# Output projection on four PSUM banks, residual tokens in other places of SBUF, and the first FFN products ahead of the last transposes

## The chip, the cores and the metric

The kernel runs on one core of a Trainium2 chip. The core has five engines with a queue of instructions each: TensorE (PE in the profile, with its weight loads as PEld), VectorE (DVE), ScalarE (ACT), GpSimd (POOL) and SyncE (SP), which here only issues transfers. They share the SBUF memory, and the matmul accumulators in PSUM, which has eight banks here, each of 512 fp32 numbers a partition. The metric is the device time of one execution in microseconds (us).

## The reference

One step of a hybrid decoder layer, for 1024 prompt tokens and 64 sample tokens (8 sequences of 8) that share the weights; the model width is 1024, the FFN width 2816. The part that the change touches is the tail of the layer, cut here to its core:

```python
# layer(): after attention, pooling and memory branches
merged = ga * (o @ w_br_attn) + gb * (pool_out @ w_br_pool) + gm * (om @ w_br_mem)
x = x + merged @ w_out                                   # output projection, residual
f, conv_state = conv_ffn(rmsnorm(x, norm2_g), conv_prefix, w_gate, w_up, conv_w, conv_b, w_down)
x = x + f

def conv_ffn(h, prefix, w_gate, w_up, conv_w, conv_b, w_down):
    g = h @ w_gate
    u = h @ w_up
    ext = concatenate([prefix, g], axis=1)
    gc = conv_b + sum(conv_w[j] * ext[:, j:j + L] for j in range(3))
    f = (gelu(gc) * u) @ w_down
    return f, ext[:, -2:]
```

All values are fp32. The outputs are the final normed tokens of both groups, keys and values, and the states.

## The kernel before, in words

**How fp32 products are made.** Each fp32 operand is split in two parts, hi and lo, by `split` (L109 ACT casts the hi part, L110 DVE subtracts it to get lo), and a product is three matmuls (`PASSES`: hi-hi, hi-lo, lo-hi) per 128 rows of the contraction. `put` takes 128 tokens by 512 columns of the normed residual, transposes them by four matmuls with the identity (L106), and splits the result into a right-hand operand of 128 by 512 tokens.

**Output projection (L917 to L994).** The residual tokens sit in eight tiles `x1[t]` of 128 tokens by 1024 columns and one tile `x1s` of 64 sample tokens; SP loads them (L949, L951) behind the weights. `w_out` is worked in two column halves, nb = 0 and 1. In each half the sample tokens come first (`mm_s`, L195, 16 matmuls) and then eight token tiles (`mm_n`, L187, 24 matmuls each). Each result bank is taken by `nat()`, which has two banks. `add_sq` adds the bank to the residual (L926, DVE), and ACT squares the sum with a running total (L927) and puts the squares, as scratch, into the same bank; only then is the bank free for the next tile but one.

In the second half each tile goes on: GpSimd's queue stores it to DRAM (L971, `x1_d`), `norm2` makes the scale (L931 and L116 to L122) and scales it in place (L933; it overwrites what the store reads, so it waits for the store to land), and `put` brings it into the FFN's operands. The FFN's gate and up products are a Strassen-like form with seven products for eight: the tokens are taken in pairs (even, odd), the columns in halves, which gives operands B11, B21 (of even tiles), B22 (of odd ones) and four more, T1 to T4, which are transposes of differences. The four differences of a pair (L982 to L985) are made in place, one after the other, two on DVE (L982, L984) and two on GpSimd (L983, L985), DVE and GpSimd in turn. T1 and T2 are filled as the pairs come; T3 and T4 are filled last, eight `put`s in `late`. Before that point `put` has two PSUM banks, called tp and av, which `tpb()` gives in turn.

**FFN gate and up (L996 to L1149).** For each of 22 blocks m of 256 weight columns (gate and up in turn), `prep(m)` makes the seven weight operands: four sums and differences on GpSimd (L1081, L1085, L1094, L1098, each into a tile `stm`, of which there are three) and seven splits (tiles wA to wD). It also does the sample tokens (`sample_ffn`: L1032, 16 matmuls per block, with a transposition of the 64 by 256 result). `products(m)` runs seven groups of 12 matmuls (L1109, `prod`) into one pair of banks `big` (halves a and b) and one bank `nat` (c): a11 on B11, s1 on T1, s2 on T2, a12 on B21, s3 on T3, s4 on B22, a22 on T4. ACT copies (`nc.scalar.copy`) and DVE additions (`acc`, L1125) bring the partial sums out of the banks. The `s3` group goes on adding into half a, and may start only when what stood there has been copied.

**What sets the order.** The program is written tile by tile, and a scheduler of the tile framework sets the order in each engine's queue; each queue then runs strictly in that order, with waits on semaphores. So the PE order of before and of the change need not be the order of the source. Pools of SBUF (`p5` for the residual tokens, `fa` for the FFN's working tiles, `pB` for the B operands) are given addresses one after the other, and a tile whose address belonged to a tile of a closed pool waits for the last use of what stood there.

Of the kernel before, what the change touches and what calls it, by code (L numbers as in the profile page):

```python
# [32 lines left out]
def hybrid_step(ctx, tc, x_prompt, x_sample, mem_prompt, cache_k, cache_v, page_table, state_pool,  # L33
# [868 lines left out]
    pB_cm = tc.tile_pool(name="pB", bufs=1, reuse_waits="tile")  # L902
# [12 lines left out]

    with tc.tile_pool(name="p5", bufs=1, reuse_waits="tile") as p5:
# [3 lines left out]
        nc.sync.dma_start(g2b, bc(norm2_g[0], P))  # L920
# [21 lines left out]
        raws = {}  # L942
        T1 = T2 = None
        todo, late = [], []
        for nb in range(2):
# [19 lines left out]
            for i, t in enumerate((0, 2, 1, 3, 4, 6, 5, 7) if nb else range(NT)):  # L965
                pt = nat()
# [15 lines left out]
                nc.vector.tensor_tensor(xa[:, 0:512], xb[:, 0:512], xa[:, 0:512], op=ALU.subtract)  # L982
                nc.gpsimd.tensor_tensor(xb[:, 0:512], xb[:, 512:D], xb[:, 0:512], op=ALU.subtract)  # L983
                nc.vector.tensor_tensor(xb[:, 512:D], xb[:, 512:D], xa[:, 0:512], op=ALU.subtract)  # L984
# [8 lines left out]
        T3, T4 = [ap_.tile([P, 2, 4, 512], F32R, tag="act", bufs=4, name=f"T{q}") for q in (3, 4)]  # L993
        for (xa, xb, a) in late:  # L994
            put(T3, xb[:, 0:512], a)
            put(T4, xa[:, 512:D], a)  # L996

    with tc.tile_pool(name="fa", bufs=1, reuse_waits="tile") as fa:
        def stm():
            return fa.tile([P, 4, P], F32, tag="stm", bufs=3, name=f"stm{uid()}")  # L1000

# [8 lines left out]
        def gu():  # L1010
            return fa.tile([P, T], F32, tag="gu", bufs=6, name=f"gu{uid()}")

        def conv(g, f):
            nc.gpsimd.tensor_copy(gc[:, f], g[:, T - 2:T])
            out = gu()
            nc.scalar.activation(out, g, AF.Identity, bias=cwb[:, f, 3:4], scale=cwb[:, f, 2:3])
            nc.vector.scalar_tensor_tensor(out[:, 1:], g[:, 0:T - 1], cwb[:, f, 1:2], out[:, 1:], op0=ALU.mult, op1=ALU.add)
            nc.vector.scalar_tensor_tensor(out[:, 2:], g[:, 0:T - 2], cwb[:, f, 0:1], out[:, 2:], op0=ALU.mult, op1=ALU.add)
            nc.scalar.activation(out, out, AF.Gelu_apprx_tanh)
            return out  # L1020

        def conv_s(out, e, f):
            nc.vector.tensor_scalar(out, e[:, :, 0:DS], cwb[:, f, 0:1], cwb[:, f, 3:4], op0=ALU.mult, op1=ALU.add)
            nc.vector.scalar_tensor_tensor(out, e[:, :, 1:1 + DS], cwb[:, f, 1:2], out, op0=ALU.mult, op1=ALU.add)
            nc.vector.scalar_tensor_tensor(out, e[:, :, 2:2 + DS], cwb[:, f, 2:3], out, op0=ALU.mult, op1=ALU.add)

        def sample_ffn(m, raw):
            j, c0 = m // 2, (m // 2) * 256
            pt = tpb()
            for k in range(KT):  # L1030
                r = (k % 2) * TS
                nc.tensor.matmul(pt[r:r + TS, 0:256], xs[:, k, 0:TS], raw[k // 4][:, k % 4], start=(k < 2), stop=(k >= 6),  # L1032
                                 tile_position=(0, r))
            gs = fa.tile([TS, 256], F32, tag="gs", bufs=2, name=f"gs{m}")
            nc.scalar.copy(gs, pt[TS:P, 0:256])
# [258 lines left out]
```

## Time and profile before

| what | value |
|---|---|
| median of 3 runs | 1833.76 us (1833.25 to 1834.86) |
| the profiled execution's own time | 1830.01 us |
| its span (first to last instruction in the profile) | 1828.2 us |
| PE busy | 1746.8 us, 96% of the span |
| DVE, ACT, POOL busy | 902.6, 716.9, 390.3 us |
| granted TensorE clock, mean | 0.98 of full |

The page divides the span into 40 slices of 45.7 us; the output projection and the start of the FFN lie between 918 and 1085 us, in the slices 21 to 24. A row of the timeline gives the start, the busy time, the engine, the line, what is written and read, the count, and in brackets how long the engine had been idle before and who released it. Names in rows leave out buffer numbers: `x` is one of the residual tiles, `B` and `T` the FFN's operands, `hl` a split weight tile, `nat`, `big`, `tp`, `av` the PSUM banks. "PEclk" in a table of windows is the granted clock of TensorE in that window, as a share of full speed.

### The profile page before, as it was taken

To read this page: it belongs to the slowest core of one execution; us is meant where nothing else is said; L and a number is where in the kernel's file an instruction comes from. 1 tells how busy PE (TensorE), PEld (TensorE's weight loads), DVE (VectorE), ACT (ScalarE), POOL (GpSimd) and SP (SyncE) were. 2 spreads that over 40 slices of the span, in tenths; PEclk is the share of its full clock that TensorE was granted. 3 is DMA by queue.
4 is the path that set the end of the run, shared out by engine and by line. 5 is a ranking of instruction groups with operands and counts; after the bars stand their busy time and mean duration, and the time that the engine had idled before them with its cause. 6 is when DMAs were issued, how large, how long until landed. Compare 5 with 4: busy or idle time off the path is not lost.

```text
span 1828.2 us, 22933 instructions
## 1 busy us (share of the span) xinstructions
PE 1746.8 (96%) x8285; PEld 1337.9 (73%) x8285; DVE 902.6 (49%) x1543; ACT 716.9 (39%) x1397; POOL 390.3 (21%) x427
## 2 busy tenths in 40 slices
PE   7999999998999999969989799999999999999997
PEld 5887876765776777747768667777777777788876
DVE  6421135221121676666725776666666666436464
ACT  5331235231221666655413353333334434334343
POOL 1113020302001242102200244443333342000000
PEclk9999999999999999969989999999999999999999
DMA  7341260557566342154442132222222223746663
GB/s 278 132 149 57 82 198 24 150 186 247 195 199 189 90 123 77 55 164 141 162 155 75 58 60 70 70 71 70 70 71 70 70 71 118 248 140 208 206 218 117
DMA packets 137367, 234.74 MB, mean 128 GB/s; under 512 B 25679, under 2 KB 71533, under 8 KB 137253
## 3 DMA queue, kind: packets, MB, share of 16 engines
q1 hardware_dynamic: 122117, 187.16, 32.3%
q0 software_dynamic: 15136, 46.12, 6.7%
q8 instruction: 65, 1.06, 0.2%
q14 instruction: 49, 0.40, 0.1%
HBM read 182.74 MB, written 50.54 MB: 128 GB/s over the span
## 4 chain that ended last, share of the span: by engine, by line
PE 78%; issue 8%; DVE 5%; DMA 4%; ACT 2%; POOL 2%; SPq 1%; POOLq 0%; DVEq 0%; ACTq 0%
PE big L1109 17%; PE nat L178 15%; PE big L1222 10%; PE nat L1109 7%; PE nat L187 5%; PE big L178 4%; PE nat L1222 3%; PE tp L1032 3%; PE tp L106 3%; PE av L106 2%; PE av L805 2%; PE nat L195 2%; PE big L775 1%; PE av L542 1%; DMA raw<-in_w_in 1%
## 5 line engine op out<-in xcount | busy, mean ns | idle before, releaser
L178 PE MATMUL nat<-act,hl 128*128 128x512 f32 x1344 | 352.1, 402 | 0.0
L178 PEld LDWEIGHTS nat<-act,hl 128*128 128x128 f32 x1344 | 243.2, 188 | 63.9 <-issue 14.0
L187 PE MATMUL nat<-hl,act 128*128 128x512 f32 x768 | 186.1, 400 | 9.9 <-ACT nat L927 8.2
L1222 PE MATMUL big<-wd,fh 128*128 128x512 f32 x792 | 187.5, 390 | 4.1 <-ACT big L1190 2.5
L187 PEld LDWEIGHTS nat<-hl,act 128*128 128x128 f32 x768 | 146.2, 192 | 42.0 <-ACT nat L927 8.6
L1222 PEld LDWEIGHTS big<-wd,fh 128*128 128x128 f32 x792 | 148.3, 188 | 36.3 <-ACT big L1190 3.4
L110 DVE TENSOR_TENSOR hl<-raw,hl 128x1024 fp32r<-128x1024 f32 x52 | 66.7, 1291 | 162.6 <-ACT hl L109 161.0
L1109 PE MATMUL big<-B,wA 128*128 128x512 f32 x528 | 130.6, 395 | 0.0
L110 DVE TENSOR_TENSOR wd<-wr,wd 128x1024 fp32r<-128x1024 f32 x66 | 84.5, 1282 | 74.0 <-ACT wd L109 71.9
L1109 PEld LDWEIGHTS big<-B,wA 128*128 128x128 f32 x528 | 97.4, 188 | 28.0 <-ACT gu L1134 8.2
L109 ACT CAST wd<-wr 128x1024 fp32r<-128x1024 f32 x66 | 69.3, 1052 | 83.2 <-PE tps L1229 35.3
L110 DVE TENSOR_TENSOR wB<-stm,wB 128x512 fp32r<-128x512 f32 x44 | 50.4, 1147 | 73.4 <-ACT wB L109 73.4
L568 POOL DMA_DIRECT2D gl<-ev x48 | 26.2, 545 | 272.0 <-ACT ev L567 244.7
L567 ACT COPY ev<-nat 128x512 f32<-128x512 f32 x48 | 28.1, 585 | 130.3 <-PE nat L178 130.1
L109 ACT CAST hl<-raw 128x1024 fp32r<-128x1024 f32 x60 | 62.6, 1051 | 26.7 <-DMA raw<-in_w_in 10.6
L1109 PE MATMUL nat<-B,wC 128*128 128x512 f32 x264 | 69.9, 399 | 0.0
L1163 POOL TENSOR_TENSOR gu<-gu,gu 128x1024 f32<-128x1024 f32 x22 | 57.0, 2590 | 52.3 <-DVE gu L1125 22.5
L1222 PE MATMUL nat<-wd,fh 128*128 128x512 f32 x264 | 67.2, 389 | 0.0
L1109 PE MATMUL big<-T,wD 128*128 128x512 f32 x264 | 66.7, 401 | 0.0
L1098 POOL TENSOR_TENSOR stm<-rf,stm 128x512 f32<-128x512 f32 x22 | 28.6, 1300 | 169.6 <-DVE wB L110 169.6
L1109 PE MATMUL big<-T,wC 128*128 128x512 f32 x264 | 64.6, 393 | 0.0
L1109 PE MATMUL nat<-T,wB 128*128 128x512 f32 x264 | 64.1, 390 | 0.0
(420 smaller groups left out, 3089.5 us busy)
## 6 DMA issues: line engine op xcount, KB each, us to landing
wr<-in_w_ffn_down SPq DMA_DIRECT2D x66, 512.0 KB
raw<-in_w_in SPq DMA_DIRECT2D x40, 512.0 KB
kr<-in_cache_k SPq DMA_DIRECT2D x64, 256.0 KB
vr<-in_cache_v SPq DMA_DIRECT2D x64, 256.0 KB
gl<-ev POOLq DMA_DIRECT2D x48, 256.0 KB, 3.1
rf<-in_w_ffn_gate SPq DMA_DIRECT2D x22, 512.0 KB
rf<-in_w_ffn_up SPq DMA_DIRECT2D x22, 512.0 KB
f_d<-gu POOLq DMA_DIRECT2D x22, 512.0 KB, 3.0
```

The costliest lines, as they stand in the source:

```text
L106: nc.tensor.transpose(out, in_, ident[:n, :n])
L109: nc.scalar.copy(hi, src)
L110: (lo_eng or nc.vector).tensor_tensor(lo, src, hi.bitcast(F32), op=ALU.subtract)
L178: nc.tensor.matmul(out, wf(k, pw)[:, n0:n0 + P], acts[c][ph][:, k, :], start=(k == ks[0] and (pw, ph) == (0, 0)), stop=(k == ks[-1] and (p ...
L187: nc.tensor.matmul(out, acts[c][ph][:, k, o:o + P], wf(k, pw), start=(k == ks[0] and (pw, ph) == (0, 0)), stop=(k == ks[-1] and (pw, ph) = ...
L195: nc.tensor.matmul(out, stack[:, k, :], wf(k, pw), start=(k == ks[0] and pw == 0), stop=(k == ks[-1] and pw == 1))
L805: nc.tensor.matmul(av[:, :P], aT[:, k * P:(k + 1) * P], vn[:, k0 + k], start=(k0 + k == 0), stop=(k0 + k == i))
L1032: nc.tensor.matmul(pt[r:r + TS, 0:256], xs[:, k, 0:TS], raw[k // 4][:, k % 4], start=(k < 2), stop=(k >= 6), tile_position=(0, r))
L1098: nc.gpsimd.tensor_tensor(s4, a12, s2, op=ALU.subtract)
L1109: nc.tensor.matmul(out, wt[:, pw, k], Bt[:, ph, k], start=(start and k == 0 and (pw, ph) == (0, 0)), stop=(k == 3 and (pw, ph) == (1, 0)), ...
L1163: nc.gpsimd.tensor_tensor(g[i], g[i], gts[i], op=ALU.mult)
L1222: nc.tensor.matmul(banks[i][nb], fh[:, ph, kk, i * P:(i + 1) * P], wh[:, pw, nb * 512:(nb + 1) * 512], start=(k == 0 and (pw, ph) == (0, 0 ...
```

## The change

Five things are done at once.

1. **Four banks for the projection.** `x1s` and the token tiles take their banks from `big()`, which has two pairs; two token tiles share one pair, and `x1s` takes the second half of a pair of its own. The sequence of pairs is x1s, (t0, t1), (t2, t3), and so on.
2. **`put` on four banks.** `put` takes in turn a bank of `nat()` and one of `tpb()`.
3. **Other homes.** `x1_5`, `x1_6`, `x1_7` are placed first in `p5`, then `x1s`, then the other tiles; `pB` moves to the other side of SBUF, so that `p5` and `fa` begin at other addresses; the load of the norm's gain `g2b` is written behind the loads of `x1`.
4. **Differences.** In all pairs but the last, all four differences are made by GpSimd; in the last pair (6, 7) they remain divided between DVE and GpSimd.
5. **Early products.** `prep` splits a12 together with a11, and `products` has a form `early` in which the groups a11 on B11 and a12 on B21 come first. For m = 0 and m = 1 these two groups (48 matmuls) are written ahead of the eight `put`s of T3 and T4. The helpers `stm`, `gu`, `conv`, `sample_ffn`, `prep`, `products` move ahead of the projection, unchanged but for this; the change in `g` at the end only fetches the two blocks begun early.

```diff
-    pB_cm = tc.tile_pool(name="pB", bufs=1, reuse_waits="tile")
+    pB_cm = tc.tile_pool(name="pB", bufs=1, side="right", reuse_waits="tile")
...
         tA = pair("wA")
         w["a11"] = piece(tA, 0, a11)
+        w["a12"] = piece(tA, 1, a12)
         yield
...
-            w["a12"] = piece(tA, 1, a12)
             smp_ = sample_ffn(m, raw)
...
+    def products(m, nxt, early=False):
...
         prod(a, w["a11"], B11, True)
+        if early:
+            prod(b, w["a12"], B21, True)
+            yield
+        g0, g1 = gu(), gu()
         nc.scalar.copy(hv(g0, 0), q(a))
...
-            prod(b, w["a12"], B21, True)
+        if not early:
+            prod(b, w["a12"], B21, True)
         acc(g0, 0, b)
...
     with tc.tile_pool(name="p5", bufs=1, reuse_waits="tile") as p5:
-        x1 = [p5.tile([P, D], F32, name=f"x1_{t}") for t in range(NT)]
+        x1 = [p5.tile([P, D], F32, name=f"x1_{t}") for t in (5, 6, 7)]
         x1s = p5.tile([TS, D], F32, name="x1s")
+        x1 = [p5.tile([P, D], F32, name=f"x1_{t}") for t in range(5)] + x1
         g2b = p5.tile([P, D], F32, name="g2b")
-        nc.sync.dma_start(g2b, bc(norm2_g[0], P))
...
+        pc = [0]
+
         def put(Bt, xh, a):
-            pt = tpb()
+            pc[0] += 1
+            pt = nat() if pc[0] % 2 else tpb()
...
             else:
+                nc.sync.dma_start(g2b, bc(norm2_g[0], P))
                 raws[0], raws[1] = raw_ffn(0), raw_ffn(1)
-            pt = nat()
-            mm_s(pt, wf, ms)
+            pt2 = big()
+            pt = pt2[:, 1]
+            mm_s(pt2[:, 1], wf, ms)
...
-                pt = nat()
+                if i % 2 == 0:
+                    pt2 = big()
+                pt = pt2[:, i % 2]
                 mm_n(pt, wf, macts, t)
...
-                nc.vector.tensor_tensor(xa[:, 0:512], xb[:, 0:512], xa[:, 0:512], op=ALU.subtract)
+                ve = nc.vector if i == 7 else nc.gpsimd
+                ve.tensor_tensor(xa[:, 0:512], xb[:, 0:512], xa[:, 0:512], op=ALU.subtract)
                 nc.gpsimd.tensor_tensor(xb[:, 0:512], xb[:, 512:D], xb[:, 0:512], op=ALU.subtract)
-                nc.vector.tensor_tensor(xb[:, 512:D], xb[:, 512:D], xa[:, 0:512], op=ALU.subtract)
+                ve.tensor_tensor(xb[:, 512:D], xb[:, 512:D], xa[:, 0:512], op=ALU.subtract)
                 nc.gpsimd.tensor_tensor(xa[:, 512:D], xa[:, 512:D], xb[:, 512:D], op=ALU.subtract)
...
         T3, T4 = [ap_.tile([P, 2, 4, 512], F32R, tag="act", bufs=4, name=f"T{q}") for q in (3, 4)]
+        pp = [prep(m) for m in range(2)]
+        pend = []
+        for m in range(2):
+            next(pp[m])
+            pend.append(products(m, prep(2) if m else pp[1], True))
+            next(pend[m])
         for (xa, xb, a) in late:
             put(T3, xb[:, 0:512], a)
             put(T4, xa[:, 512:D], a)
...
         for m in range(2 * NG):
-            nxt = prep(m + 1) if m + 1 < 2 * NG else iter(())
-            g = products(m, nxt)
-            for _ in nxt:
-                pass
+            g = next(pend[m] if m < 2 else products(m, prep(m + 1) if m + 1 < 2 * NG else iter(())))
```

The order that the scheduler makes of this is shown at three places. In these rows each name has its buffer number; the bracket lists the semaphores that the instruction waits on, by their owner.

**PE in the first column half, around the end of token tile 0.** `big1195`, not in the rows, holds the sample tokens' product, `nat1196` and `big1196` are the banks of token tiles 0 (and, with the change, 1); before, in `nat1195` stood the sample tokens' product. Before:

```order
L187 MATMUL nat1196_8897<-hl1194_8865,act1067_7999 128x512 x2
L187 MATMUL nat1196_8897<-hl1194_8865,act1068_8000 128x512
L187 MATMUL nat1196_8897<-hl1194_8865,act1067_7999 128x512
L187 MATMUL nat1197_8924<-hl1188_8850,act1067_7999 128x512 [waits Activation_49]
L187 MATMUL nat1197_8924<-hl1188_8850,act1068_8000 128x512
L187 MATMUL nat1197_8924<-hl1188_8850,act1067_7999 128x512 x2
```

With the change:

```order
L187 MATMUL big1196_8896<-hl1194_8864,act1067_7999 128x512 x2
L187 MATMUL big1196_8896<-hl1194_8864,act1068_8000 128x512
L187 MATMUL big1196_8896<-hl1194_8864,act1067_7999 128x512
L187 MATMUL big1197_8949<-hl1188_8849,act1067_7999 128x512 [waits Activation_49]
L187 MATMUL big1197_8949<-hl1188_8849,act1068_8000 128x512
L187 MATMUL big1197_8949<-hl1188_8849,act1067_7999 128x512 x2
L187 MATMUL big1196_8896<-hl1188_8849,act1067_7999 128x512 [waits Activation_49]
```

Before, token tile 1 follows tile 0 in the bank of x1s's product. With the change four matmuls of tile 2 (`big1197`, the pair that held x1s's product) stand between tile 0 and tile 1, and the first of them waits for ACT.

**GpSimd in the second column half, from the store of tile 5 to the first sum of FFN weights.** L971 and L1126 are the stores, L983 and L985 and L1138 to L1141 the differences, L1081 and L991 the first weight sum. Before:

```order
L971 DMA x1_d5_8822<-x1_5_8841 128x1024 [waits DMAHW6_49,DVE_49]
L971 DMA x1_d7_8824<-x1_7_8843 128x1024 [waits DMAHW0_49,DMASW5_49,DVE_49]
L983 TENSOR_TENSOR x1_5_8841<-x1_5_8841 128x512 [waits DVE_49]
L985 TENSOR_TENSOR x1_4_8840<-x1_4_8840,x1_5_8841 128x512 [waits DVE_49,Activation_49]
L983 TENSOR_TENSOR x1_7_8843<-x1_7_8843 128x512 [waits DVE_49]
L985 TENSOR_TENSOR x1_6_8842<-x1_6_8842,x1_7_8843 128x512 [waits DVE_49,PE_49,Activation_49]
L1081 TENSOR_TENSOR stm1286_9745<-rf00_9133,rf01_9135 128x512 [waits DMAHW1_49,PE_49,Pool_49]
```

With the change:

```order
L1126 DMA x1_d5_8822<-x1_5_8836 128x1024 [waits DMAHW5_49,DVE_49]
L1138 TENSOR_TENSOR x1_4_8844<-x1_5_8836,x1_4_8844 128x512 [waits DVE_49,PE_49]
L1139 TENSOR_TENSOR x1_5_8836<-x1_5_8836 128x512 [waits Pool_49]
L1140 TENSOR_TENSOR x1_5_8836<-x1_5_8836,x1_4_8844 128x512 [waits PE_49,Activation_49,Pool_49]
L1141 TENSOR_TENSOR x1_4_8844<-x1_4_8844,x1_5_8836 128x512 [waits Pool_49]
L1126 DMA x1_d7_8824<-x1_7_8838 128x1024 [waits DMAHW7_49,DMASW5_49,DVE_49]
L1139 TENSOR_TENSOR x1_7_8838<-x1_7_8838 128x512 [waits DVE_49]
L1141 TENSOR_TENSOR x1_6_8837<-x1_6_8837,x1_7_8838 128x512 [waits DVE_49]
L991 TENSOR_TENSOR stm1282_9800<-rf00_9129,rf01_9131 128x512 [waits DMAHW1_49,PE_49,Pool_49]
```

Before, the store of tile 7 stood ahead of all differences of pair (4, 5); now it stands behind four of them. The wait on PE of the first weight sum is, by the addresses, for the fourth of the eight late transposes before, and for the last of them (of tile 6) with the change.

**PE and DVE at the start of the FFN.** On PE, with the change, from the last projection matmul of tile 7 (`big1255`) to the first late transpose (`nat1274`); `big1270` is block 0, `big1272` block 1, and where a line is left out, three `put`s of the last pair stand between block 1's products:

```order
L187 MATMUL big1255_9533<-hl1207_9125,act1069_8001 128x512
L1018 MATMUL big1270_9671<-B11_8830,wA0_9666 128x512 [waits Activation_49]
L1018 MATMUL big1270_9671<-B11_8830,wA0_9666 128x512 x11
L1018 MATMUL big1270_9671<-B21_8831,wA0_9666 128x512 [waits Activation_49]
L1018 MATMUL big1270_9671<-B21_8831,wA0_9666 128x512 x11
L1018 MATMUL big1272_9706<-B11_8830,wA1_9701 128x512 [waits Activation_49]
...
L1018 MATMUL big1272_9706<-B11_8830,wA1_9701 128x512 x5
L1018 MATMUL big1272_9706<-B21_8831,wA1_9701 128x512 x12
L106 MATMUL nat1274_9732<-ident_72,x1_1_8841 128x128 [waits PE_49]
L106 MATMUL nat1274_9732<-ident_72,x1_1_8841 128x128 x3
```

Before, only the twelve matmuls of a11 on B11 of block 0 stood there. On DVE, from the first split of block 1's `wB` to the addition (`acc`) for which PE's group s3 of block 0 waits; before:

```order
L110 TENSOR_TENSOR wB1_9839<-stm1296_9840,wB1_9839 128x512 [waits Activation_49]
L110 TENSOR_TENSOR wB1_9839<-stm1297_9857,wB1_9839 128x512 [waits Activation_49]
L1036 TENSOR_TENSOR gs1_9885<-tp1298_9876,gs1_9885 64x256 [waits Activation_49]
L1125 TENSOR_TENSOR gu1294_9804<-gu1294_9804,big1292_9802 128x4x128 [waits PE_49]
L110 TENSOR_TENSOR wC1_9901<-stm1299_9902,wC1_9901 128x512 [waits Activation_49]
L110 TENSOR_TENSOR wC1_9901<-stm1300_9919,wC1_9901 128x512 [waits Activation_49]
```

With the change (the six rows of `fsv`, L932 to L934, between the third and the fourth are the sample tokens' convolution):

```order
L110 TENSOR_TENSOR wB1_9858<-stm1290_9859,wB1_9858 128x512 [waits Activation_49]
L110 TENSOR_TENSOR wB1_9858<-stm1291_9876,wB1_9858 128x512 [waits Activation_49]
L110 TENSOR_TENSOR wC1_9906<-stm1293_9907,wC1_9906 128x512 [waits Activation_49]
...
L110 TENSOR_TENSOR wC1_9906<-stm1294_9924,wC1_9906 128x512 [waits Activation_49]
L1033 TENSOR_TENSOR gu1288_9855<-gu1288_9855,big1270_9671 128x4x128 [waits Activation_49]
L945 TENSOR_TENSOR gs1_9902<-tp1292_9893,gs1_9902 64x256 [waits Activation_49]
```

Before, the addition stood ahead of both splits of block 1's `wC`; with the change it stands behind them, and these need the last of block 1's weight sums.

More of the change, by code (lines that the diff above doesn't have):

```diff
@@ L914, in raw_ffn, with stm, gu, conv @@
         return out
+    def stm():
+        return fa.tile([P, 4, P], F32, tag="stm", bufs=3, name=f"stm{uid()}")
+    def gu():
+        return fa.tile([P, T], F32, tag="gu", bufs=6, name=f"gu{uid()}")
+    def conv(g, f):
+        nc.gpsimd.tensor_copy(gc[:, f], g[:, T - 2:T])
+        out = gu()
+        nc.scalar.activation(out, g, AF.Identity, bias=cwb[:, f, 3:4], scale=cwb[:, f, 2:3])
+        nc.vector.scalar_tensor_tensor(out[:, 1:], g[:, 0:T - 1], cwb[:, f, 1:2], out[:, 1:], op0=ALU.mult, op1=ALU.add)
+        nc.vector.scalar_tensor_tensor(out[:, 2:], g[:, 0:T - 2], cwb[:, f, 0:1], out[:, 2:], op0=ALU.mult, op1=ALU.add)
+        nc.scalar.activation(out, out, AF.Gelu_apprx_tanh)
+        return out
@@ L1008, in hybrid_step @@
             nc.sync.dma_start(cwb[:, :, 3], ffn_conv_b[0].rearrange("(f p) -> p f", p=P))
[L1010 to L1020, printed above, removed]
@@ L1150, in hybrid_step @@
-        for _ in prep(0):
+        for _ in pp[0]:
             pass
@@ L1174, in hybrid_step @@
     pB_cm.__exit__(None, None, None)
-    with tc.tile_pool(name="fb", bufs=1, reuse_waits="tile") as fb:
+    with tc.tile_pool(name="fb", bufs=1, side="right", reuse_waits="tile") as fb:
         fr_b = [fb.tile([P, 2, 384], F32, name=f"fr{i}") for i in range(3)]
```

229 lines of the change are left out of this document (113 added, 116 removed).

## The prediction

> **What bounds the kernel now.** I read the page first: busy time, slices, and the chain that ended last.
>
> ```profile
> PE 1746.8 (96%) x8285; PEld 1337.9 (73%) x8285; DVE 902.6 (49%) x1543; ACT 716.9 (39%) x1397; POOL 390.3 (21%) x427
> PE   7999999998999999969989799999999999999997
> PE 78%; issue 8%; DVE 5%; DMA 4%; ACT 2%; POOL 2%; SPq 1%; POOLq 0%; DVEq 0%; ACTq 0%
> ```
>
> PE is the bound, so time can only come from where it stands still or runs at a lower clock. The change works between 918 and 1085 us, where the slices dip to 6. The timelines and windows of that stretch show two gaps; from 1059.6 on PE has none.
>
> ```profile
> 920.96 5.64 PE L187 MATMUL nat<-hl,act 128*128 128x512 f32 x24
> 934.76 1.65 PE L187 MATMUL nat<-hl,act 128*128 128x512 f32 x3 [8.16 <-ACT nat L927]
> 920.00:929.90 9.90, 6.46 (x27) 4.99 (x27) 3.12 (x5) 0.62 (x1) 0.00 (x0) 1.00 0.87 248
> 929.90:940.00 10.10, 5.24 (x12) 4.13 (x13) 2.06 (x3) 1.33 (x4) 0.00 (x0) 0.50 0.98 374
> 975.40:1033.80 58.40, 55.77 (x274) 44.99 (x274) 40.29 (x94) 18.15 (x44) 9.54 (x12) 1.00 0.26 94
> 1033.80:1042.50 8.70, 4.94 (x29) 3.57 (x27) 8.21 (x16) 2.58 (x7) 3.06 (x3) 1.00 0.15 61
> 1042.50:1059.60 17.10, 13.03 (x56) 9.00 (x56) 10.02 (x16) 8.48 (x15) 6.91 (x6) 0.50 0.37 5
> 1059.60:1085.00 25.40, 25.40 (x119) 18.87 (x116) 20.67 (x27) 14.34 (x27) 12.44 (x12) 1.00 0.28 85
> ```
>
> In a window row stand the window, its length, the busy time of PE, PEld, DVE, ACT and POOL, the granted clock, the DMA share and GB/s. **Gap 1:** token tile 0 ends at 926.6, and tile 1 waits 8.16 us for ACT's square of the sample tokens, which stands in its bank. The clock falls to 0.50 about 3.3 us after the stop: 12 matmuls took 5.24 us, 0.437 each. What the square waits for:
>
> ```profile
> 921.85 0.37 SPq L912 DMA_DIRECT2D rf<-in_w_ffn_gate  x1
> 922.45 0.34 SPq L920 DMA_DIRECT2D g2b<-in_norm_g  x1
> 922.85 0.48 SPq L949 DMA_DIRECT2D x1s<-in_x_sample  x1
> 928.72 0.33 SPq L951 DMA_DIRECT2D x<-in_x_prompt  x1
> 931.04 0.33 SPq L951 DMA_DIRECT2D x<-in_x_prompt  x1
> 932.38 0.33 SPq L951 DMA_DIRECT2D x<-in_x_prompt  x1
> SPq L951 <- DMA g2b<-in_norm_g: 2.0, 1, 2.0
> 932.41 1.40 DVE L926 TENSOR_TENSOR x1s<-x1s,nat 64x512 f32<-64x512 f32 x2 [8.60 <-DMA x1s<-in_x_sample]
> 933.98 0.59 ACT L927 ACTIVATE nat<-x1s 64x512 f32<-64x512 f32 x1 [10.90 <-DVE x1s L926]
> ```
>
> Three late issues of L951 go out as rf, g2b and x1s have landed: 928.7, 931.0, 932.4. So x1s lands last of three transfers, and from there to the next matmul pass 2.4 us (add, square). **Gap 2** begins at the end of the projection:
>
> ```profile
> 1033.67 2.43 PE L1109 MATMUL big<-B,wA 128*128 128x512 f32 x10
> 1039.30 0.63 PE L106 MATMUL tp<-ident,x 128*128 128x128 f32 x4 [1.82 <-DVE B L110]
> 1041.83 0.63 PE L106 MATMUL av<-ident,x 128*128 128x128 f32 x4 [1.90 <-DVE x L933]
> 1055.42 1.08 PE L106 MATMUL av<-ident,x 128*128 128x128 f32 x4 [0.64 <-POOL stm L1094]
> 1072.65 3.01 PE L1109 MATMUL big<-T,wC 128*128 128x512 f32 x12
> ```
>
> After the first products only transposes are left, on two banks, each waiting for the last tile's norm, its differences, or the split that frees a bank; from 1042.5 the clock is 0.50 here too. The last transposes end at 1056.5. The group s3 of block 0 starts at 1072.65: I use it as the mark to measure the change by.
>
> **The change part by part.** *Four banks and the load of g2b.* In the changed PE order, four matmuls of tile 2 in x1s's own pair stand ahead of tile 1, so PE still waits for the same square: the four banks don't free it here. On SP's queue the load of g2b moves behind the token loads, while the one of rf stays ahead. What is gained is g2b's time, 931.04 − 928.72 = **2.3 us**; x1s lands at 930.0, PE goes on at 932.4, and the stop of 5.8 us still halves the clock. Bounds: 0, if the token loads, now issued earlier, take that time, and 8.16 + 12 × (0.437 − 0.227) = 10.7, if PE could pass the square.
>
> *put on four banks, and the order in the second half.* Before, PE is idle 58.40 − 55.77 = 2.6 us there. The price of a transposition, and of a matmul at full clock:
>
> ```profile
> 991.51 0.60 PE L106 MATMUL tp<-ident,x 128*128 128x128 f32 x4
> 991.95 0.60 PE L106 MATMUL av<-ident,x 128*128 128x128 f32 x4
> 992.30 4.60 PE L187 MATMUL nat<-hl,act 128*128 128x512 f32 x19
> 1083.03 2.88 PE L1109 MATMUL nat<-T,wB 128*128 128x512 f32 x12
> 1085.75 0.62 PE L1109 MATMUL big<-T,wB 128*128 128x512 f32 x2
> ```
>
> Two transpositions take 0.79 us from 991.51 to 992.30, 0.40 each; twelve matmuls 2.72 us, 0.227 each. Three more transpositions stand ahead of the projection's end in the changed order: **+1.2 us**, moved only. The first matmul of tile 0 now waits for the square of tile 7 from the first half, **+0.6** (the square of 933.98 took 0.59).
>
> *Differences on GpSimd.* Rows beside each other:
>
> ```profile
> 1004.94 0.68 DVE L982 TENSOR_TENSOR x<-x,x 128x512 f32<-128x512 f32 x1
> 1005.87 1.30 POOL L983 TENSOR_TENSOR x<-x 128x512 f32<-128x512 f32 x1
> 1005.87 1.32 DVE L931 TENSOR_TENSOR ss<-ssn 128x1 f32<-128x1 f32 x1 [0.25 <-ACT nat L927]
> 1021.79 0.56 POOL L971 DMA_DIRECT2D x_d<-x  x1 [3.42 <-DVE x L926]
> 1025.62 1.28 DVE L933 SCALAR_TENSOR_TENSOR x<-x,rsy,g2b 128x1024 f32<-128x1024 f32 x1 [1.29 <-DMA x_d<-x]
> ```
>
> A difference is 1.30 us on GpSimd against 0.68 on DVE, so four in line are 5.2 us. Before, the pair from 1004.94 ended at 1010.3, 5.4 us with the handing over; the pair itself is no later. But the stores of tiles 3 and 7 now stand behind a whole pair in GpSimd's queue, tile 4's amid one, and from a store's issue to the scaling that waits for it are 3.8 us; the transpositions and PE come behind that. Also a DVE addition of one column with two SBUF inputs, whose like takes 0.16, took 1.32 beside the GpSimd difference that began with it. Bounds: nothing, if the store finds GpSimd free, and 7.8 = three stores, each behind half a pair (2.6). I take the middle, **+3.9 us**, as no row is nearer to either end. The projection then ends at 1033.8 − 2.3 + 1.2 + 0.6 + 3.9 = 1037.2.
>
> [...]
>
> *Early products.* 48 matmuls instead of 12 stand ahead of the late transpositions: 48 × 0.227 = 10.9 us. Three transpositions of the last pair among them (1.2), a stall for that pair's norm (0.5; before 1.90) and eight late ones on four banks make 16.6. Of these eight I take four at 0.40, with a bank free, and four at the pace of the split that frees one, 0.6 (DVE's 0.68, overlapping a little): 4.0. Before, on two banks and at half clock, ten intervals from 1041.83 to 1055.42 took 13.6, 1.4 each. So the last transposes end at 1037.2 + 16.6 = 1053.8.
>
> What follows hangs on GpSimd: the weight sums' tiles now lie where tiles 5 to 7 stood, and the first waits for the very last transposes, while before the first ran at 1051.49, five us ahead of them. The scheduler also puts the addition for which group s3 waits behind both splits of block 1's wC, so all eight sums must be made first.
>
> ```profile
> 1051.49 1.27 POOL L1081 TENSOR_TENSOR stm<-rf,rf 128x512 f32<-128x512 f32 x1 [5.09 <-issue]
> 1059.00 1.60 POOL L1098 TENSOR_TENSOR stm<-rf,stm 128x512 f32<-128x512 f32 x1 [3.66 <-DVE wB L110]
> 1059.38 1.77 DVE L110 TENSOR_TENSOR wC<-stm,wC 128x512 fp32r<-128x512 f32 x1
> 1063.94 1.15 POOL L1046 DMA_DIRECT2D out<-gs  x2
> 1071.90 0.69 DVE L1125 TENSOR_TENSOR gu<-gu,big 128x512 f32<-128x512 f32 x1 [0.59 <-PE big L1109]
> ```
>
> Where both engines work, a sum and a split go in turn, near 1.7 us a pair: 8 × 1.7 = 13.6, stores 1.15, the last split 1.3 (cast and subtraction, 0.6 and 0.7), the addition 0.7: **16.7 us** (14.3 if the sums go at 1.27 as alone, 18.5 if the three tiles for sums hold GpSimd up once more). Group s3 starts at 1070.5. Before, it started at 1072.65, but without 24 of the early matmuls (5.4) and with 5 of group s4 done (1.1): the same work was done at 1077.0. The lead is **6.5 us**.
>
> *What it costs later.* PE has some 10 us of work in those 16.7 (two blocks of sample matmuls, T1, T2), so it stands about 6. That may halve the clock once: 12 matmuls more at 0.437, **2.5 us** (0 to 5), and block 1's s3 can wait similarly, **1.2** (0.5 to 2.5). From block 2 on PE has the same order and no gaps; the other pool sides change no queue: 0.
>
> Sum: 6.5 − 2.5 − 1.2 = 2.8 us gained: 1830.0 becomes 1827.2 for the profiled execution. The runs' median lies 3.8 above it, so 1833.76 − 2.8 = **1831.0 us**.
>
> [...]
>
> **The rivals.**
> *A clean win.* GpSimd's chains are hidden (+0 instead of 3.9), the sums go at 1.27 (14.3 instead of 16.7), the clock stays and block 1 doesn't wait: 2.8 + 3.9 + 2.4 + 3.7 = 12.8 us gained, **1821.0**. For it: POOL is busy 9.54 of 58.40 us in the second half; against it: 1.60 and 1.77 beside each other.
> *Gap 1 doesn't shrink.* The token loads fill what g2b leaves, since the queues are at 0.98 of their share there: 0.5 gained, **1833.3**.
> *Slower.* GpSimd's queue decides: stores behind differences hold tiles 3, 4 and 7 back by 2.6 each (−3.9), the chain after the last transposes takes 18.5 (−1.8), and the idle time halves the clock for two such stretches (−2.5): 2.8 − 8.2 = −5.4, **1839.2**. It decides as soon as the three stores together come more than 6.7 us late at PE (3.9 + 2.8).
>
> **How the numbers follow.** The forecast has 0.45, the clean win 0.22, no smaller gap 0.14, slower 0.19. A measurement tells 0.2% (3.7 us) from no change here. The forecast's own range is 1827 to 1835; of its 0.45, 0.19 lie below 1830.1. Faster: 0.22 + 0.19 = 0.41; slower: 0.19 + 0.01 = 0.20; the same: 0.39. The range 1822 to 1838.5 leaves out half of the clean win and half of the slower case.
>
> **What would show it.** Right, if the stop after tile 0 is still there at some 5.8 us; the stores of tiles 3 and 7 start late behind L1141; the first L991 starts with the end of the last transposes, near 1054, and s3 of block 0 follows 16 to 17 us later behind an addition that DVE makes after wC. Wrong, if gap 1 vanishes, if DVE's splits aren't longer beside GpSimd's, or if s3 starts before 1066 or after 1076.

## The result, and the profile after

The changed kernel takes 1845.05 us (median of 5 runs, 1841.87 to 1848.76) against 1833.25 us, a ratio of **1.0064 [1.0047, 1.0081]**: slower by 0.64%, where 2.8 us of gain were forecast. Its profiled execution took 1841.87 us (span 1840.1), 11.9 us more than the one of before. One of the nine runs of e3 below is a slow one (2465.22 us at a mean granted clock of 0.652) and stays out of its ratio.

Busy time and the chain on the page of the changed kernel, which answer to those of before:

```profile
PE 1757.0 (95%) x8285; PEld 1335.8 (73%) x8285; DVE 903.1 (49%) x1537; ACT 717.3 (39%) x1397; POOL 400.8 (22%) x433
PE 82%; DVE 5%; DMA 4%; issue 3%; ACT 3%; POOL 2%; SPq 1%; DVEq 0%; POOLq 0%; ACTq 0%
```

PE has as many matmuls as before, and is busy 10.2 us longer: it does not only wait more, it works more slowly somewhere. Rows from the timeline of PE in the stretch that the change rewrites, with others between them left out:

```profile
920.19 5.64 PE L187 MATMUL big<-hl,act 128*128 128x512 f32 x24
930.84 34.96 PE L187 MATMUL big<-hl,act 128*128 128x512 f32 x144 [5.00 <-ACT big L1076]
1005.00 0.66 PE L106 MATMUL av<-ident,x 128*128 128x128 f32 x4 [1.16 <-POOL x L1140]
1011.95 0.66 PE L106 MATMUL nat<-ident,x 128*128 128x128 f32 x4 [0.70 <-POOL x L1138]
1027.26 1.19 PE L187 MATMUL big<-hl,act 128*128 128x512 f32 x4 [1.53 <-ACT big L1076]
1033.81 0.66 PE L106 MATMUL av<-ident,x 128*128 128x128 f32 x4 [1.00 <-POOL x L1138]
1036.85 1.11 PE L106 MATMUL nat<-ident,x 128*128 128x128 f32 x4 [1.68 <-POOL x L1140]
1039.46 6.68 PE L1018 MATMUL big<-B,wA 128*128 128x512 f32 x27
1056.20 0.63 PE L106 MATMUL av<-ident,x 128*128 128x128 f32 x4
1076.00 5.26 PE L1018 MATMUL big<-T,wC 128*128 128x512 f32 x12 [4.18 <-DVE gu L1033]
1118.93 2.92 PE L1018 MATMUL big<-T,wC 128*128 128x512 f32 x12
1550.42 3.03 PE L1018 MATMUL big<-T,wC 128*128 128x512 f32 x12
```

The last two rows are group s3 of block 2 and of block 21. In the kernel before they start so:

```profile
1117.26 2.93 PE L1109 MATMUL big<-T,wC 128*128 128x512 f32 x12
1545.51 3.01 PE L1109 MATMUL big<-T,wC 128*128 128x512 f32 x12
```

From block 2 on the order on PE is the same in both. PE doesn't stop again before FFN-down, and there it stops three times in either kernel, 4.08 us together before and 3.93 after. Yet the way to block 21 takes 431.49 us against 428.25, and from there to the end of the span 289.7 against 282.7. These two differences, 3.2 and 7.0, are **10.2 us of the 11.9**, far behind the place that the change is about. The table shows where each kernel's time lies, each from the rows of one profile (starts of the stages as in the timeline above; e1, e4, e8 and e10 are experiments below):

| stage, us | before | after | e1 | e4 | e8 | e10 |
|---|---|---|---|---|---|---|
| tile 0 to the transposes of x1s | 64.8 | 62.7 | 64.5 | 64.0 | 53.8 | 54.2 |
| to the first product (a11) | 47.9 | 56.6 | 56.6 | 50.3 | 49.6 | 48.2 |
| to the end of the last transposes | 22.8 | 17.4 | 17.3 | 18.7 | 18.7 | 22.9 |
| to s3 of block 0 | 16.2 | 19.2 | 19.2 | 19.2 | 17.2 | 16.1 |
| to s3 of block 2 | 44.6 | 42.9 | 42.7 | 42.3 | 40.5 | 44.6 |
| sum to here | 196.3 | 198.7 | 200.4 | 194.5 | 179.8 | 186.0 |
| to s3 of block 21 | 428.3 | 431.5 | 428.3 | 428.3 | 428.2 | 428.3 |
| to the end of the span | 282.7 | 289.7 | 282.8 | 284.3 | 282.7 | 282.7 |

The 284.3 of e4 is no effect of its edit: behind a stop of 1.81 us in FFN-down, which before, e1 and e2 have there too (1.77 in the changed kernel and e3), 264 matmuls took 61.73 us, against 60.13 before and 60.14 in e1. The 1.6 us more are what some 3.2 us at a clock of 0.50 would lose, an estimate from these times. Six of the fourteen profiles show a loss of this size, and the others don't: e2 (61.76 us), and e4, e6, e9, e11 and e12, which take 712.5 to 712.7 us from s3 of block 2 to the end of the span, where before, e1, e5, e7, e8 and e10 take 710.9 to 711.0.

### The profile page after: what moved, and what is told of

Same layout as the page of the kernel before. It is cut to its first block, busy times and chain, and to the rows that moved or that the text cites. A ratio compares the mean times of both kernels' runs of the same rounds, so it can differ in the third digit from the quotient of the medians.

```text
span 1840.1 us, 22926 instructions
## 1 busy us (share of the span) xinstructions
PE 1757.0 (95%) x8285; PEld 1335.8 (73%) x8285; DVE 903.1 (49%) x1537; ACT 717.3 (39%) x1397; POOL 400.8 (22%) x433
## 4 chain that ended last, share of the span: by engine, by line
PE 82%; DVE 5%; DMA 4%; issue 3%; ACT 3%; POOL 2%; SPq 1%; DVEq 0%; POOLq 0%; ACTq 0%
PE big L1018 16%; PE nat L178 15%; PE big L1238 10%; PE nat L1018 7%; PE nat L187 5%; PE big L187 4%; PE big L178 4%; PE nat L1238 3%; PE tp L941 3%; PE tp L106 3%; PE nat L195 2%; PE av L106 2%; PE av L805 1%; PE big L775 1%; PE av L542 1%
## 5 line engine op out<-in xcount | busy, mean ns | idle before, releaser
L1238 PE MATMUL big<-wd,fh 128*128 128x512 f32 x792 | 192.6, 396 | 3.9 <-ACT big L1206 2.4
L187 PE MATMUL big<-hl,act 128*128 128x512 f32 x384 | 94.8, 402 | 7.7 <-ACT big L1076 7.7
L187 PE MATMUL nat<-hl,act 128*128 128x512 f32 x384 | 92.9, 400 | 1.8 <-DVE act L110 1.0
L187 PEld LDWEIGHTS big<-hl,act 128*128 128x128 f32 x384 | 72.3, 192 | 25.4 <-ACT big L1076 10.8
L187 PEld LDWEIGHTS nat<-hl,act 128*128 128x128 f32 x384 | 73.4, 193 | 18.4 <-DVE act L110 1.8
L109 ACT CAST hl<-raw 128x1024 fp32r<-128x1024 f32 x60 | 62.6, 1051 | 26.7 <-PE nat L178 10.1
```

The lines of the kernel that those rows point to most:

```text
L109: nc.scalar.copy(hi, src)
L187: nc.tensor.matmul(out, acts[c][ph][:, k, o:o + P], wf(k, pw), start=(k == ks[0] and (pw, ph) == (0, 0)), stop=(k == ks[-1] and (pw, ph) = ...
L1238: nc.tensor.matmul(banks[i][nb], fh[:, ph, kk, i * P:(i + 1) * P], wh[:, pw, nb * 512:(nb + 1) * 512], start=(k == 0 and (pw, ph) == (0, 0 ...
```

## The experiments

### The slower matmuls: place or alignment (e1, e2, e3)

One block of the FFN and one step of FFN-down, in the kernel before:

```profile
1170.79 2.88 PE L1109 MATMUL big<-B,wA 128*128 128x512 f32 x12
1173.51 2.88 PE L1109 MATMUL nat<-T,wB 128*128 128x512 f32 x12
1604.22 2.88 PE L1222 MATMUL big<-wd,fh 128*128 128x512 f32 x12
1606.94 1.52 PE L1222 MATMUL nat<-wd,fh 128*128 128x512 f32 x6
1608.30 0.61 PE L1229 MATMUL av<-wd,fs 128*128 128x512 f32 x2
```

and in the changed kernel:

```profile
1172.82 2.97 PE L1018 MATMUL big<-B,wA 128*128 128x512 f32 x12
1175.62 2.92 PE L1018 MATMUL nat<-T,wB 128*128 128x512 f32 x12
1605.23 2.96 PE L1238 MATMUL big<-wd,fh 128*128 128x512 f32 x12
1608.03 1.56 PE L1238 MATMUL nat<-wd,fh 128*128 128x512 f32 x6
1609.43 0.62 PE L1245 MATMUL av<-wd,fs 128*128 128x512 f32 x2
```

Twelve matmuls on B11 take 2.80 us from start to start instead of 2.72, and 18 on `fh` 4.20 instead of 4.08: 0.0067 us more for each of these, at the same granted clock (1.00 from 1100 to 1800 us in both). The two products on `fs` beside them hardly changed (0.61 and 0.62). A whole FFN block, with its 36 products on B, takes 0.17 us more: the twelve on B21 lose 0.02 us and those on B22 0.04, where those on B11 lose 0.08, and the twelve on T1 behind B11 lose 0.04 us together though T1 lies where it lay. B and `fh` are what lies in the pools that moved to the other side, `pB` and also `fb`, the pool of FFN-down, which got `side="right"` too: B11 starts at byte 180192 of a partition instead of 138176, `fh0` at 190432 instead of 147392. Two things differ: they lie at the far end, and the new addresses are 32 over a multiple of 64.

e1, the changed kernel with padding:

```diff
-    B11, B21, B22 = [pB.tile(...) ...]
+    B11, B21, B22 = [pB.tile(...) ...]; pB.tile([P, 8], F32, name="pad_b")
...
-        gfb = fb.tile([P, D], F32, name="gfb")
+        gfb = fb.tile([P, D], F32, name="gfb"); fb.tile([P, 8], F32, name="pad_f")
```

> The changed kernel with 32 bytes of padding at the end of the pools pB and fb, which sit at the far side of SBUF: B11, B21, B22 and the fh tiles then start at multiples of 64 bytes (B11 at 180160 instead of 180192), still at the far side; the order on every engine is unchanged. Theory A (a matmul operand that starts 32 bytes off a multiple of 64 costs more): twelve matmuls on B11 take 2.72 us again instead of 2.80, a step of FFN-down 4.99 instead of 5.11, and the time falls by about 10.5 us, 22 blocks x 0.17 = 3.7 and 7.0 in FFN-down, to about 1834.5. Theory B (the far side of SBUF is slower, or shares something with other traffic there): unchanged, near 1845.

Measured: 1838.53 us (10 runs), 1.0026 [1.0017, 1.0035] of before. The rates are those of before, at the far side:

```profile
1180.01 2.88 PE L1018 MATMUL big<-B,wA 128*128 128x512 f32 x12
1182.73 2.88 PE L1018 MATMUL nat<-T,wB 128*128 128x512 f32 x12
1603.42 2.88 PE L1238 MATMUL big<-wd,fh 128*128 128x512 f32 x12
1606.14 1.52 PE L1238 MATMUL nat<-wd,fh 128*128 128x512 f32 x6
1607.50 0.61 PE L1245 MATMUL av<-wd,fs 128*128 128x512 f32 x2
```

Both late stages are back to 428.3 and 282.8 us. The ratio fell by 0.0038, 7.0 us, with an interval of about 3.5 us to either side (the two intervals together), which holds the stages' 10.2 at its edge; a part of the rest is that the early stages of e1's profile are 1.7 us longer than those of the changed kernel, in the stop after tile 0. So the far side itself costs these products nothing: 2.72 and 4.08 us from start to start again.

e2 and e3, the same from the other end, on the kernel before:

```diff
# e2
+    pB.tile([P, 8], F32, name="pad_b"); B11, B21, B22 = ...; pB.tile([P, 8], F32, name="pad_c")
# e3
+        fb.tile([P, 8], F32, name="pad_f"); fh_b = [...]; fb.tile([P, 8], F32, name="pad_g")
```

> The kernel before, with B11, B21 and B22 moved up by 32 bytes at their old place (138208 instead of 138176), everything behind them by 64 bytes, the order unchanged. Theory A: the groups on B11 take 2.80 us, a block of FFN gate or up 0.17 us more, 22 of them 3.7 us: about 1837. Theory B: unchanged, 1833.3.

> The kernel before, with only the three fh tiles of FFN-down moved up by 32 bytes (147424 instead of 147392), the tiles behind by 64, the order unchanged. These are the stationary operands. Theory A: 1056 matmuls at 0.0067 us more each, 7.0 us: about 1840.3. Theory B: unchanged, 1833.3.

Measured: e2 1836.68 us, 1.0018 [1.0009, 1.0027]; e3 1840.43 us, 1.0034 [1.0023, 1.0045]. That is +3.3 and +6.2 us by the ratios, where theory A expected 3.7 and 7.0. The rows of e2, then of e3:

```profile
1173.86 2.97 PE L1109 MATMUL big<-B,wA 128*128 128x512 f32 x12
1176.66 2.92 PE L1109 MATMUL nat<-T,wB 128*128 128x512 f32 x12
```

```profile
1603.84 2.96 PE L1222 MATMUL big<-wd,fh 128*128 128x512 f32 x12
1606.64 1.56 PE L1222 MATMUL nat<-wd,fh 128*128 128x512 f32 x6
```

In e2 only B is off, in e3 only `fh`, each at its old place, and each shows the rates of the changed kernel, 2.80 us for twelve from start to start. So it is the 32 bytes, for the moving operand (B, 512 columns) as for the stationary one (`fh`, 128 columns). Theory B falls.

### The differences on GpSimd (e4)

This edit stands on e1, and all further experiments but e10 stand on e4:

```diff
-                ve = nc.vector if i == 7 else nc.gpsimd
+                ve = nc.vector
```

> The kernel of e1 with the differences of all pairs divided between DVE and GpSimd, as in the kernel before. Theory C (four differences in line on GpSimd hold PE up in the second half of the projection): the five waits of PE that the changed kernel's trace gives to L1138 and L1140, 1.16, 0.70, 0.55, 1.00 and 1.68 us, 5.1 together, shrink to about 2, and the kernel is some 3 us faster than e1. Theory D (PE waits as long for the norm and for DVE in their stead): within 1 us of e1.

Measured: 1832.97 us, 0.9999 [0.9990, 1.0008] of before, so 5 us faster than e1 (0.0027, with some 2.3 us to either side). The stage from the sample tokens' transposes to the first product shrinks from 56.6 to 50.3 us, and no wait on L1138 or L1140 of GpSimd is left on PE there; what is left is for the norm, at most 1.07 us, and the wait in the pair of banks:

```profile
1021.57 0.66 PE L106 MATMUL nat<-ident,x 128*128 128x128 f32 x4 [1.07 <-DVE x L1082]
1029.69 0.97 PE L187 MATMUL big<-hl,act 128*128 128x512 f32 x3 [1.53 <-ACT big L1076]
1075.09 4.83 PE L1018 MATMUL big<-T,wC 128*128 128x512 f32 x12 [5.19 <-DVE gu L1033]
```

Theory C holds. A part of the 6.3 us is the clock: in the changed kernel it is 0.50 from 1036.5 to 1039.9, behind the wait of 1.68 us, and not in e4 (1.00 from 1030 to 1045). With e1 and e4 the change costs nothing any more, and gains nothing: the other edits together are worth 0, within 2 us.

### The chain behind the last transposes (e5) and the early products (e6)

The rows of GpSimd and DVE that lead to group s3 in the changed kernel:

```profile
1056.96 1.27 POOL L991 TENSOR_TENSOR stm<-rf,rf 128x512 f32<-128x512 f32 x1 [7.80 <-issue]
1061.24 1.71 POOL L1007 TENSOR_TENSOR stm<-rf,stm 128x512 f32<-128x512 f32 x1
1066.79 3.10 DVE L110 TENSOR_TENSOR wB<-stm,wB 128x512 fp32r<-128x512 f32 x2
1075.27 0.68 DVE L1033 TENSOR_TENSOR gu<-gu,big 128x512 f32<-128x512 f32 x1
```

The first sum starts with the end of the last transposes, 1056.8, and DVE's addition comes 18.3 us later. e5 moves only the tiles, so that the sums lie over tiles whose late transposes come first:

```diff
-        x1 = [p5.tile([P, D], F32, name=f"x1_{t}") for t in (5, 6, 7)]
+        x1 = {t: p5.tile([P, D], F32, name=f"x1_{t}") for t in (3, 1, 0)}
         x1s = p5.tile([TS, D], F32, name="x1s")
-        x1 = [p5.tile([P, D], F32, name=f"x1_{t}") for t in range(5)] + x1
+        x1.update({t: p5.tile([P, D], F32, name=f"x1_{t}") for t in (2, 4, 5, 6, 7)})
```

> The kernel of e4 with tiles 3, 1 and 0 at the places of 5, 6 and 7, so that the FFN's weight sums take the places of the two tiles whose late transposes come first, not last; the order on every engine is unchanged. In e4 the last transposes end at 1055.9 and group s3 of block 0 starts 19.2 us later. Theory E (the eight sums can begin only when their places are free, and this sets s3): the sums begin some 3.5 us earlier, s3 too, and the time falls by 3 to 5 us, to about 1829. Theory F (DVE, whose queue has all splits of the late transposes ahead of the sums' splits, or the rows behind set s3): within 1 us of e4.

Measured: 1828.09 us, 0.9973 [0.9963, 0.9983], some 4.8 us less than e4 by the ratios. GpSimd begins 3.3 us ahead of the last transposes' end (1050.37 against 1053.7), and s3 comes 17.2 us behind that end, 2.0 earlier than in e4:

```profile
1050.37 1.28 POOL L991 TENSOR_TENSOR stm<-rf,rf 128x512 f32<-128x512 f32 x1 [4.42 <-issue]
1056.20 1.61 POOL L1007 TENSOR_TENSOR stm<-rf,stm 128x512 f32<-128x512 f32 x1 [1.97 <-DVE wB L110]
```

Theory E holds in its main point, and F in part: the fourth sum waits 1.97 us for DVE, whose queue has the late transposes' splits first. The profile shows 2.7 us of gain to block 2 (191.8 against 194.5), the runs more.

e6 leaves the early products out:

```diff
         w["a11"] = piece(tA, 0, a11)
-        w["a12"] = piece(tA, 1, a12)
         yield
...
+        w["a12"] = piece(tA, 1, a12)
         smp_ = sample_ffn(m, raw)
...
-            next(pp[m])
-            pend.append(products(m, prep(2) if m else pp[1], True))
-            next(pend[m])
+            pend.append(products(m, prep(2) if m else pp[1]))
```

> The kernel of e4 without the early products: a12 is split at its old place and both blocks' products follow the late transposes, with everything else kept. Theory G (the 36 matmuls more ahead of the late transposes fill time in which PE would stand, 8.2 us of work): 4 to 8 us slower than e4, about 1838. Theory H (they only move the standing to behind the transposes, where PE waits for the sums): within 1.5 us of e4.

Measured: 1831.46 us, 0.9991 [0.9982, 0.9999]. Without them PE stands for the last tile's norm,

```profile
1044.86 1.08 PE L106 MATMUL tp<-ident,x 128*128 128x128 f32 x4 [3.32 <-DVE x L1082]
```

but block 2 is reached in 194.6 us from tile 0 against 194.5 in e4, and the runs differ by 1.5 us, within their uncertainty. Theory H holds: with the sums as late as they are, the early products only move the standing to 5.19 us ahead of s3.

### The stop after tile 0 (e7, e8, e10, e12)

In the changed kernel's order, the second tile in a pair waits for the square of the first one in the same pair, and the first of the next pair for the sample tokens' square; two pairs act as two tiles. e7 gives each its own tile in the first half:

```diff
-            pt2 = big()
-            pt = pt2[:, 1]
-            mm_s(pt2[:, 1], wf, ms)
+            pt2 = big() if nb else None
+            pt = pt2[:, 1] if nb else nat()
+            mm_s(pt, wf, ms)
...
-                if i % 2 == 0:
-                    pt2 = big()
-                pt = pt2[:, i % 2]
+                if i % 2 == 0 or not nb:
+                    pt2 = big() if nb or i % 2 == 0 else None
+                pt = pt2[:, i % 2] if pt2 is not None else nat()
```

> The kernel of e4 with the first half's banks taken as four tiles in turn, nat for the sample tokens, then one half of a big pair, nat, and so on, so that neither tile 0, 1 nor 2 uses the bank of the sample tokens, and no two token tiles share a pair; the second half is unchanged. Theory I (PE stands 5.1 us only because the first matmul of the next pair waits for the sample tokens' square, and the second half of a pair waits for the square in the first): the stop after tile 0 is gone, and with it the lower clock behind it; 5 to 8 us less than e4, about 1826.5. Theory J (the stop moves to where the next load or square comes late): within 2 us of e4.

Measured: 1820.36 us, 0.9931 [0.9915, 0.9946]; 12.5 us less than e4 by the ratios, more than the 5 to 8 of theory I, with 10 us in the profile's first stage (64.0 to 53.8). The stop is gone, and the clock stays at 1.00 from 920 to 940:

```profile
923.09 5.61 PE L187 MATMUL big<-hl,act 128*128 128x512 f32 x24
928.54 5.60 PE L187 MATMUL nat<-hl,act 128*128 128x512 f32 x24
933.98 5.60 PE L187 MATMUL big<-hl,act 128*128 128x512 f32 x24
```

Theory J falls. What I had left out are the squares' waits at two later places, 0.63 and 0.65 us in e4, and the full price of the slow matmuls behind the stop: in e4 the next matmul starts at 933.7, 10.8 us behind tile 0's first instead of 5.4, and the 39 from there to 945 take 11.7 us, 2.8 more than at 0.227.

e8 is e5 and e7 together.

> The edits of e5 and e7 together on e4. If both stops are apart in time, the two gains add: 8 to 13 us less than e4, about 1822, faster than the kernel before by 0.6%. If one of the theories E and I falls, what the other alone gives.

Measured: **1816.49 us, 0.9917 [0.9900, 0.9935]**, faster than both kernels, and by the ratios 15.0 us less than e4; the two gains alone, 4.8 and 12.5, add up to 17.3, the same within the uncertainty. The stop ahead of s3 is 2.07 us, and s3 goes at full clock, twelve matmuls in 3.03. But behind an earlier stop of 1.93 us ten matmuls took 4.05 us, where the same ten took 2.59 in e5; the mean clock from 1040 to 1100 was 0.97:

```profile
1054.60 0.29 PE L106 MATMUL av<-ident,st 16*128 16x16 f32 x2 [1.93 <-DMA st<-in_state_ffn_conv]
1054.82 4.05 PE L1018 MATMUL big<-T,wB 128*128 128x512 f32 x10
1062.87 3.03 PE L1018 MATMUL big<-T,wC 128*128 128x512 f32 x12 [2.07 <-DVE gu L1033]
```

e10 puts the four tiles alone on the kernel before:

```diff
-                pt = nat()
+                pt = nat() if nb or i % 2 else big()[:, 0]
```

> The kernel before with one edit: in the first half the token tiles take in turn half of a big pair and a nat bank, the sample tokens nat, so that four tiles of PSUM go round; everything else, the load of g2b too, as before. If gap 1 is bought by banks alone: 8.2 us of standing and about 2.5 us of lower clock less, 10.7 us, to about 1822.5. If it takes the later load of g2b too: the stop moves behind tile 2 or shrinks by half, about 1828.

Measured: 1822.82 us, 0.9945 [0.9931, 0.9958]: 10.1 us from one line, the load of g2b as it was. So the bound that the prediction gave for "if PE could pass the square", 10.7, was right in size.

e12 puts the load of g2b in e4 back ahead of the tokens:

```diff
         g2b = p5.tile([P, D], F32, name="g2b")
+        nc.sync.dma_start(g2b, bc(norm2_g[0], P))
...
             else:
-                nc.sync.dma_start(g2b, bc(norm2_g[0], P))
```

> The kernel of e4 with the load of g2b at its old place, ahead of the sample tokens on SP's queue. If its transfer is what delayed the sample tokens: the stop after tile 0 grows from 5.1 to 5.9 us to about 7.4 to 8.2, 2.3 us more, to about 1835.3 (the clock may take 1 to 2 us more). If not: within 1 us of e4.

Measured: 1835.48 us, 1.0014 [1.0005, 1.0024], 2.7 us more than e4 by the ratios; the stop grows from 5.12 to 9.18 us:

```profile
940.86 1.65 PE L187 MATMUL big<-hl,act 128*128 128x512 f32 x3 [9.18 <-ACT big L1077]
```

The runs agree with the 2.3 us for g2b's transfer. The stop in this one profile grew by more, 4.1 us, but it is not steady: 5.00 to 6.62 us in the five profiles with the later load (the changed kernel, e1, e4, e5, e6), 7.91 to 8.50 in the three of the order of before (before, e2, e3).

### What the rest is worth on the best kernel (e9, e11)

e9 is e8 without the early products (the edit of e6), e11 is e8 with `put` on two banks:

```diff
-            pt = nat() if pc[0] % 2 else tpb()
+            pt = tpb()
```

> The kernel of e8 without the early products, as in e6. In e6 they were worth nothing (1831.5 without, 1833.0 with), since PE then waited for the sums behind the late transposes in either case. Theory H2 (with the sums begun earlier the early products fill time again): 3 to 6 us slower than e8, about 1820.5. Theory H (they still only move the standing): within 1.5 us of e8, or faster.

> The kernel of e8 with put on the two banks of the kernel before. If four banks for the transposes are worth something: the eight late transposes go at 1.3 us each instead of 0.6, 5 us, some of it hidden by the sums: 2 to 5 us slower than e8. If the sums set the end alone: within 1.5 us of e8.

Measured: e9 1820.88 us, 0.9932 [0.9915, 0.9950]; e11 1821.83 us, 0.9939 [0.9924, 0.9954]. Against e8 that is +2.8 and +4.0 us by the ratios, each with some 4.5 us of uncertainty; in the profiles block 2 comes 1.8 and 4.3 us later from tile 0 than in e8. For four banks of `put` both readings point to some 4 us, the runs no further than their uncertainty. For the early products the sign is that of theory H2, but 1.8 to 2.8 us against this uncertainty don't settle it.

## Why the prediction was wrong

**The step that failed** is "From block 2 on PE has the same order and no gaps; the other pool sides change no queue: 0". The order was the same, and the gaps too (three short ones in FFN-down), but the price of a matmul was taken to be independent of where its operands lie. The operands in the moved pools start 32 bytes off a multiple of 64, and that made 3.2 us up to block 21 (0.17 a block) and 7.0 in FFN-down (0.0067 on each of 1056 products with `fh`) in the profile (e1, e2, e3). With 0 in this place the forecast could not have come out slower by this much; none of the rivals had it either. It isn't the whole miss: without it, e1 is still 4.8 us slower than before by the ratio. The second half and the chain to s3 were mis-sized as well.

Step by step, the others:

- *The load of g2b, 2.3 us.* Right by the runs: putting it back (e12) costs 2.7 us, with some 2.4 to either side. The profiles scatter: the stop fell from 8.16 to 5.00 us and the first stage by 2.1, with the square's wait (0.63, forecast as 0.6) and a second one of 0.51 in it, but in e1, e4, e5 and e6, which have the same order there, the stage is shorter by only 0.3 to 1.1. "The four banks don't free it here" was right too, and e7 and e10 show what they could have done.
- *Second half, +1.2 and +3.9.* The stage grew by 8.7 us instead of 5.1. The term for the differences was mis-sized: taking them back (e4) shortens the stage by 6.3, inside the bounds of 0 and 7.8. The mechanism was only partly mine: the rows name L1138 and L1140 themselves, the transposes of T1 and T2 wait for the four differences in line (1.16, 0.70, 0.55, 1.00 and 1.68 us), where I had argued with the stores behind them. Of the three stores, that of tile 7 was not held by them at all: it goes out at 1040.69, after GpSimd has stood 2.55 us for DVE's addition. And the wait of 1.53 us in the pair of banks had no place in the sum.
- *The products and late transposes, 16.6 us.* Near: 17.4.
- *The chain to s3, 16.7 us.* 19.2, a little over its upper bound of 18.5. That the sums begin with the end of the last transposes, and that DVE's addition behind wC releases s3, is what the rows show. The pace near 1.7 us (1.71 and two splits in 3.10) was about right; the addition also stood behind the sample tokens' convolution (`fsv`, from 1071.48 to 1074.7), which I had not put into the sum. The lead at s3 was therefore 1076.96 − 920.96 − (1076.00 − 920.19) = 0.2 us instead of 6.5. (The lower bound of 14.3 doesn't follow from its own terms: 8 × 1.27 + 1.15 + 1.3 + 0.7 = 13.3.)
- *The cost later, 3.7 us.* From the mark to block 2 the kernel before took 1117.26 − 1076.96 = 40.3 us, the changed one 42.9: 2.6. The clock did fall: after the stop of 4.18 us the twelve matmuls of s3 took 5.26 (0.50 from 1074.1 to 1080.9). It had also fallen before that, from 1063.8 to 1067.2, after a stop of only 2.05:

```profile
1063.89 0.47 PE L106 MATMUL av<-ident,gs 64*128 64x64 f32 x2 [2.05 <-DVE gs L945]
1064.29 2.07 PE L1018 MATMUL nat<-T,wB 128*128 128x512 f32 x4
```

In the stop of 4.18 us the clock fell 2.3 us after it began (1071.8), in the stop of 2.05 us at its end. A short stop can bring the lower clock, and need not: in e8 s3 went at full clock after 2.07 us, twelve matmuls in 3.03.

Together the early part lost 2.4 us to block 2 where 2.8 were to be gained, and the late part lost 10.2. The tile-0 mark came 0.8 earlier in the changed kernel's profile: 2.4 + 10.2 − 0.8 = 11.8, the difference of the two profiles (11.9) but for rounding. Of the 5.2 us that the early part missed, the second half has 3.6, the chain 2.5 and the products 0.8, while the cost later (1.1) and the first stage (0.4) came out better than forecast; that these add up to 5.4 and not 5.2 is the rounding of the marks.

The third rival, "slower", had the right sign. Its 18.5 us for the chain was near the 19.2, its 7.8 for the differences near the 6.3 of e4, though not by the stores, and the lower clock in two stretches is in the trace, though the cost later stayed at 2.6. With its 5.4 us the kernel would be at 1839.2. That is near e1's 1838.5, the change without its alignment loss; since its single terms differ from the measured ones, the nearness is in part luck.

## What to carry to other kernels

Look at the start address of each matmul operand whenever a pool moves: an edit that changes neither order nor work can change the rate of the products on it (here from 0.227 to as much as 0.233 us each), and only the start-to-start times of the same group in both traces show it, not the gaps. Banks that are to free a waiting PE must be tiles of their own, since two halves of one tile waited for each other here (a stop of 5.12 us in e4, none in e7); one such line was worth more (10 us) than the whole set of edits. Before work is placed ahead of a wait, ask what the wait itself hangs on: here the tiles' places had tied it to the very end of the work put in front.

## What the runs showed of the hardware

A product whose moving operand of 512 fp32 columns (B11), or whose stationary operand of 128 (`fh`), starts 32 bytes over a multiple of 64 took 0.0067 us longer, 0.233 instead of 0.227 us from start to start; at multiples of 64, at the old place and at the far side (e1), it showed no such loss. Only this one offset was tried. Why it costs just as much on either operand, and less on B21 and B22 (0.02 and 0.04 us for twelve, against 0.08 on B11), stays open.

The granted clock fell to 0.50 for 3.4 us also behind stops of PE of only about 2 us in the changed kernel: 1.68 (from 1036.5 to 1039.9) and 2.05 (from 1063.8 to 1067.2). Ten matmuls behind a stop of 1.93 us in e8 took 4.05 us instead of e5's 2.59, and 264 behind one of 1.81 us in FFN-down of e4 61.73 instead of 60.13. With the same stop of 1.81 us e1 took 60.14, so the length of the stop alone doesn't decide it; what does stays open.
